# The second of the four late token sums, moved up to directly behind the first

## The chip, the cores and the metric

One core of a Trainium2 chip runs the whole kernel. The metric is the device time of one launch in microseconds (us). It is the median of several executions; one more execution was recorded by the hardware profiler, and all rows below come from that one.

## What is computed

One decoder layer on 512 tokens of width 2048, all in float32. The change lies where the gated MLP goes from its up projection to its down projection:

```
x = x + rmsnorm(token_mixer(rmsnorm(x, g1)), g2)
h = rmsnorm(x, g3)
up = h @ w_ffn_in                     # 512 x 11264: a | b, 5632 columns each
a  = conv_w[0]*a[t-2] + conv_w[1]*a[t-1] + conv_w[2]*a[t] + conv_b
f  = (gelu(a) * b) @ w_ffn_out        # 5632 -> 2048
y  = x + rmsnorm(f, g4)
```

## The kernel before, in words

**Products.** Each float32 operand is split into a high and a low part of a reduced type, and each product is three TensorE matmuls (high by high, high by low, low by high). Both projections of the MLP also use a Winograd-Strassen scheme: a 2 x 2 block product is made from seven products of sums of blocks, with the segments x0, z0, y0, z1, x1, y1 and y2. Each segment is two granules of 512 KB of weights. `granule` (line 129) splits one on ScalarE (line 138) and VectorE (line 139).

**Token sums.** The left operands of the seven down products are blocks of the hidden activations (a11, a12, a22) and four sums of them: s5 = a21 - a22, s2 = s5 - a11, s7 = a11 - a21, s3 = s2 - a12. They are made per group of 512 hidden columns by `token_sums`: each sum is one VectorE instruction (line 1373) on 128 x 512 float32, followed by a "put", a 256 KB transfer from the SyncE queue into DRAM (the tensors sd0 to sd4, line 48 is the helper that issues it). The four results share a tag with two buffers, and s2 reads s5, s3 reads s2. Nine groups make all four at once; the tenth group, whose sums are wanted last (they belong to sd4), keeps them as `late_sums`, to be made in the change-over.

**The change-over.** From the last up unit u to the first down units d0 and d1 the order is written out by hand in `change_over`: d0 x0, then u's y1, x1, y2, then d0's z0, y0, z1, x1, then d1's x0, then d0's y1 and y2, two granules each. `run_in_order` walks the granules. It makes a granule's halves two or three granules ahead, issues its matmuls (lines 1400 to 1402), after the second granule reads the banks out into acc (line 1406 on ScalarE, line 1408 on VectorE), and then runs the "hooks" of that granule: steps hung on a place with `at`. TensorE, ScalarE, VectorE and GpSimd keep program order here; where on its queue SyncE issues a transfer, and where instructions of the code behind the change-over (d1's z0 and its helpers at lines 1263 and 1281) are slotted in, a planner decides at build time from its own estimates.

y1 and y2 of d0 add into the same PSUM banks. So the first matmul of y2 has to wait until the read-out of y1 (two instructions at line 1408, one for each bank) is through.

**The late sums.** The four late sums hang, in the order s5, s2, s7, s3, on four places: d0 y0 first granule, d0 x1 second granule, d1 x0 first granule, d1 x0 second granule (lines 1541 and 1542).

Of the kernel before, what the change touches and what calls it, by code (L numbers as in the profile page):

```python
# [35 lines left out]
def hybrid_layer(ctx: ExitStack, tc: tile.TileContext, x, attn_pre_norm, w_in, w_alpha_up, b_alpha,  # L36
# [1416 lines left out]
    def at(u, seg, g, *fs):  # L1453
        hooks.setdefault((u, seg, g), []).extend(fs)

    def load_unit(u):
        u.t = [load_t(u.block(0, 0, g), u.a) for g in range(2)]
        u.b22, u.b21 = [], []

    def load_b(u, name, i, j, by=None):  # L1460
        getattr(u, name).extend(load(u.block(i, j, g), u.a, by) for g in range(2))

    def add_t(u, name, g):
        tt(u.t[g], u.t[g], getattr(u, name)[g], ALU.add)
# [13 lines left out]
    def prepare_at(c, n, load_at, split_at):  # L1478
        f, g = prepare_parts(c, n)
        at(*load_at, f)  # L1480
        at(*split_at, g)
# [41 lines left out]
    def change_over(u):  # L1523
        d0, d1 = downs[:2]
        order = [(d0, "x0"), (u, "y1"), (u, "x1"), (u, "y2")]
        order += [(d0, g) for g in ("z0", "y0", "z1", "x1")] + [(d1, "x0"), (d0, "y1"), (d0, "y2")]
        at(d0, "x0", 0, lambda: load_b(d0, "b22", 1, 1))
        at(d0, "x0", 0, late_tiles)
        at(d0, "x0", 1, lambda: (add_t(u, "b21", 0), add_t(u, "b21", 1)))
        at(u, "x1", 1, lambda: load_b(d0, "b21", 1, 0))  # L1530
        at(d0, "z0", 1, lambda: load_unit(d1))
        prepare_at(0, "s2", (d0, "x0", 1), (u, "y2", 0))
        prepare_at(0, "s3", (u, "y1", 1), (d0, "z0", 0))
        prepare_at(0, "a12", (u, "x1", 0), (d0, "z0", 1))
        prepare_at(0, "s7", (u, "x1", 1), (d0, "y0", 1))
        prepare_at(0, "a22", (u, "y2", 0), (d0, "z1", 1))
        for g in range(2):
            at(u, "y2", g, lambda g=g: add_t(d0, "b22", g))
        at(d0, "z1", 0, lambda: add_t(d0, "b21", 0))
        at(d0, "x1", 0, lambda: add_t(d0, "b21", 1))  # L1540
        for where in ((d0, "y0", 0), (d0, "x1", 1), (d1, "x0", 0), (d1, "x0", 1)):
            at(*where, lambda: late_sums.pop(0)())
        return order

    order = change_over(ups[-1])
    u = ups[-1]
    u.b21 = [load(u.block(1, 0, g), u.a) for g in range(2)]
# [217 lines left out]
```

## Time and profile before

| what | us |
|---|---|
| median of three executions | 2078.37 |
| lowest and highest of the three | 2074.48 and 2079.25 |
| the profiled execution, its own time | 2077.34 |
| its span in the profile | 2075.6 |
| PE (TensorE matmul) busy | 2048.7 |
| DVE (VectorE) busy | 1508.4 |
| ACT (ScalarE) busy | 1000.0 |

The profiled execution took 1.7 us more than its span. In the rows PE is TensorE, PEld its weight loads, DVE VectorE, ACT ScalarE, POOL GpSimd and SP SyncE; SPq and POOLq are the queues in which those issue transfers. L1373 is line 1373 of the kernel. A bracket at the end of a row of the timeline gives the idle time before the instruction and what ended it.

### The profile page before, as it was taken

Reading aid. Unit: us, or ns where it says so; the run is one execution under the profiler, and the core shown is the slowest. Engines: PE = TensorE matmul, PEld = TensorE weight load, DVE = VectorE, ACT = ScalarE, POOL = GpSimd, SP = SyncE. Lnnn points to the kernel's source line nnn. Section 1 sums busy time; section 2 is a strip of 40 time slices with the busy share of each in tenths; the row PEclk is TensorE's granted clock in tenths of the full one; section 3 lists DMA queues with packets and bytes.
Section 4 is the critical chain, followed back from the end, with each engine's and each line's share of the span. In section 5 each row is a group of like instructions: output and inputs, shape, how many; then the busy total and the mean of one; then the engine's idle time right before and its main releaser. Section 6 shows DMA issues by size and latency. Waiting matters only on the chain.

```text
span 2075.6 us, 35519 instructions
## 1 busy us (share of the span) xinstructions
PE 2048.7 (99%) x14429; PEld 1896.9 (91%) x14429; DVE 1508.4 (73%) x1793; ACT 1000.0 (48%) x1303; POOL 291.9 (14%) x306
## 2 busy tenths in 40 slices
PE   7999999999999999999999999999999999999998
PEld 6799999999988889899999999999999978888886
DVE  5967777666762255977777777777777888988977
ACT  5544444455552243454554554454455654544433
POOL 0112222222200000011011011111110111111100
PEclk9999999999999999999999999999999999999999
DMA  5488888888883354457667578577667886776663
GB/s 213 121 187 185 192 197 182 196 174 200 193 259 125 94 177 146 124 112 197 149 148 195 142 163 191 131 171 179 141 162 196 214 237 185 188 196 182 165 181 122
DMA packets 281465, 358.61 MB, mean 173 GB/s; under 512 B 14848, under 2 KB 223156, under 8 KB 279380
## 3 DMA queue, kind: packets, MB, share of 16 engines
q1 hardware_dynamic: 192148, 259.85, 37.4%
q0 software_dynamic: 84800, 94.38, 30.1%
q10 hardware_dynamic: 4352, 2.10, 0.4%
q8 instruction: 113, 1.85, 0.4%
q14 instruction: 52, 0.43, 0.1%
HBM read 311.72 MB, written 44.56 MB: 172 GB/s over the span
## 4 chain that ended last, share of the span: by engine, by line
PE 93%; DVE 2%; DMA 2%; issue 1%; ACT 1%; POOL 1%; DVEq 0%; SPq 0%; POOLq 0%; ACTq 0%
PE bank L1298 12%; PE bank L1299 12%; PE bank L1300 12%; PE bank L1400 6%; PE bank L1401 6%; PE bank L1402 6%; PE bank L193 3%; PE bank L192 3%; PE bank L194 3%; PE bank L793 3%; PE bank L795 3%; PE bank L794 3%; PE bank L797 2%; PE bank L798 2%; PE bank L799 2%; PE bank L176 2%
## 5 line engine op out<-in xcount | busy, mean ns | idle before, releaser
L138 ACT ACTIVATE ring<-raw 128x1024 fp32r<-128x1024 f32 x315 | 333.7, 1061 | 499.1 <-PE bank L1299 113.1
L139 DVE TENSOR_TENSOR ring<-raw,ring 128x1024 fp32r<-128x1024 f32 x315 | 383.5, 1223 | 259.3 <-ACT ring L138 256.0
L138 ACT ACTIVATE ring<-rt 128x1024 fp32r<-128x1024 f32 x221 | 234.5, 1061 | 259.3 <-PE bank L1299 154.0
L1299 PE MATMUL bank<-al,ring 128*128 128x256 f32 x1280 | 354.0, 277 | 0.0
L1298 PE MATMUL bank<-ah,ring 128*128 128x256 f32 x1280 | 354.0, 277 | 0.0
L1300 PE MATMUL bank<-ah,ring 128*128 128x256 f32 x1280 | 353.9, 277 | 0.0
L139 DVE TENSOR_TENSOR ring<-rt,ring 128x1024 fp32r<-128x1024 f32 x221 | 270.2, 1223 | 91.2 <-ACT ring L138 90.2
L1298 PEld LDWEIGHTS bank<-ah,ring 128*128 128x128 f32 x1280 | 240.5, 188 | 0.1
L1299 PEld LDWEIGHTS bank<-al,ring 128*128 128x128 f32 x1280 | 240.4, 188 | 0.1
L1300 PEld LDWEIGHTS bank<-ah,ring 128*128 128x128 f32 x1280 | 240.4, 188 | 0.0
L1402 PE MATMUL bank<-ring,al 128*128 128x512 f32 x424 | 165.8, 391 | 0.0
L1401 PE MATMUL bank<-ring,ah 128*128 128x512 f32 x424 | 165.7, 391 | 0.0
L1400 PE MATMUL bank<-ring,ah 128*128 128x512 f32 x424 | 153.2, 392 | 2.2 <-DVE acc L1408 2.2
L193 PE MATMUL bank<-ring,ah 128*128 128x512 f32 x280 | 109.8, 393 | 0.0
L192 PE MATMUL bank<-ring,ah 128*128 128x512 f32 x280 | 109.6, 397 | 0.0
L194 PE MATMUL bank<-ring,al 128*128 128x512 f32 x280 | 109.3, 393 | 0.0
L1246 POOL DMA_DIRECT2D raw<-in_w_ffn_in_dram x40 | 51.2, 1309 | 396.4 <-DVE ring L139 396.4
L1400 PEld LDWEIGHTS bank<-ring,ah 128*128 128x128 f32 x424 | 79.9, 188 | 19.7 <-DVE acc L1408 3.1
L1246 POOL DMA_DIRECT2D rt<-in_w_ffn_in_dram x40 | 50.9, 1279 | 325.9 <-DVE ring L139 303.4
L1402 PEld LDWEIGHTS bank<-ring,al 128*128 128x128 f32 x424 | 79.9, 189 | 16.7
L1401 PEld LDWEIGHTS bank<-ring,ah 128*128 128x128 f32 x424 | 79.9, 188 | 16.4
L797 PE MATMUL bank<-ring,ah 128*128 128x256 f32 x320 | 92.1, 288 | 1.0 <-ACT ah L151 1.0
(378 smaller groups left out, 5661.8 us busy)
## 6 DMA issues: line engine op xcount, KB each, us to landing
raw<-in_w_ffn_in_dram SPq DMA_DIRECT2D x96, 512.0 KB, 4.8
raw<-in_w_in_dram SPq DMA_DIRECT2D x56, 512.0 KB, 4.5
raw<-in_w_ffn_out_dram SPq DMA_DIRECT2D x46, 512.0 KB, 6.0
raw<-in_w_in_dram POOLq DMA_DIRECT2D x40, 512.0 KB, 7.2
rt<-in_w_ffn_in_dram SPq DMA_DIRECT2D x40, 512.0 KB, 6.1
rt<-in_w_ffn_in_dram POOLq DMA_DIRECT2D x40, 512.0 KB, 6.2
raw<-in_w_ffn_in_dram POOLq DMA_DIRECT2D x40, 512.0 KB, 6.9
raw<-in_w_o_dram SPq DMA_DIRECT2D x32, 512.0 KB, 3.9
```

The costliest lines, as they stand in the source:

```text
L138: act(hi, raw, AF.Copy)
L139: tt(lo, raw, hi.bitcast(F32), ALU.subtract)
L192: mm(banks[t], ah[:, t, s, :], w[0][:, k, :], start=st, stop=False)
L193: mm(banks[t], ah[:, t, s, :], w[1][:, k, :], start=False, stop=False)
L194: mm(banks[t], al[:, t, s, :], w[0][:, k, :], start=False, stop=sp)
L797: mm(o, sh[:, n, kk, :], wh[:, k, :], start=st, stop=False, **NOW)
L1298: mm(o, wh, sh[:, :, kk, :], start=start and kk == 0 and n == 0, stop=False, **NOW)
L1299: mm(o, wh, sl[:, :, kk, :], start=False, stop=False, **NOW)
L1300: mm(o, wl, sh[:, :, kk, :], start=False, stop=kk == HK - 1, **NOW)
L1400: mm(b[j], sh[:, o:o + P], w[0][:, q, :], start=start and st == 0, stop=False, **NOW)
L1401: mm(b[j], sh[:, o:o + P], w[1][:, q, :], start=False, stop=False, **NOW)
L1402: mm(b[j], sl[:, o:o + P], w[0][:, q, :], start=False, stop=st == 3, **NOW)
```

## The change

One place in one list is another: the second late sum, s2 = s5 - a11, with its put, hangs behind the first granule of d0's y0, where the first late sum hangs too, instead of behind the second granule of d0's x1. In the list of granules that is from place y0 1 to place x1 2; four whole granules lie between the two places. The third and the fourth late sum stay where they were. No instruction is added or removed.

```
-        for where in ((d0, "y0", 0), (d0, "x1", 1), (d1, "x0", 0), (d1, "x0", 1)):
+        for where in ((d0, "y0", 0), (d0, "y0", 0), (d1, "x0", 0), (d1, "x0", 1)):
             at(*where, lambda: late_sums.pop(0)())
```

## Rows read from the trace of the kernel before

**Rows 1.** The page, engines: busy us, share of the span, instructions.

```profile
PE 2048.7 (99%) x14429; PEld 1896.9 (91%) x14429; DVE 1508.4 (73%) x1793; ACT 1000.0 (48%) x1303; POOL 291.9 (14%) x306
```

**Rows 2.** Waits of PE over the run: us in total, times, longest.

```profile
PE bank L1400 <- DVE acc L1408: 2.2, 1, 2.2
PE bank L797 <- ACT ah L151: 1.0, 1, 1.0
```

**Rows 3.** Chain that ended last, 1676 to 1692: start, us, what.

```profile
1670.02 7.93 DMA sd4s<-s
...
1678.04 0.13 DVE s L1373
...
1679.79 0.69 DVE acc L1408
...
1685.18 0.39 PE bank L1400
...
1687.19 0.23 PE bank L1402
```

**Rows 4.** Stretches of 2 us: busy of each engine, granted clock, DMA share, GB/s.

```profile
1682.00:1684.00 2.00, 1.99 (x5) 1.46 (x5) 2.00 (x3) 0.00 (x0) 0.00 (x0) 0.50 0.86 316
```

**Rows 5.** Timeline of VectorE, 1652 to 1679: start, length, line, operation.

```profile
1652.83 0.69 DVE L1373 TENSOR_TENSOR s<-u 128x512 f32<-128x512 f32 x1
1654.95 1.23 DVE L152 TENSOR_TENSOR al<-st,ah 128x1024 fp32r<-128x1024 f32 x1 [1.44 <-ACT ah L151]
...
1667.57 0.69 DVE L1373 TENSOR_TENSOR s<-s,u 128x512 f32<-128x512 f32 x1
1668.17 1.22 DVE L139 TENSOR_TENSOR ring<-raw,ring 128x1024 fp32r<-128x1024 f32 x1
1669.31 0.68 DVE L1373 TENSOR_TENSOR s<-u 128x512 f32<-128x512 f32 x1
...
1673.55 1.23 DVE L139 TENSOR_TENSOR ring<-rt,ring 128x1024 fp32r<-128x1024 f32 x1 [1.29 <-ACT ring L138]
1678.04 0.69 DVE L1373 TENSOR_TENSOR s<-s,u 128x512 f32<-128x512 f32 x1 [3.27 <-DMA sd4s<-s]
```

**Rows 6.** Timeline of the SyncE queue: transfers issued, 1656 to 1671.

```profile
1656.21 0.32 SPq L48 DMA_DIRECT2D st<-sd1a  x1
...
1668.28 0.34 SPq L48 DMA_DIRECT2D sd4s<-s  x1
1669.42 0.37 SPq L102 DMA_DIRECT2D raw<-in_w_ffn_out_dram  x1
1670.02 0.34 SPq L48 DMA_DIRECT2D sd4s<-s  x1
```

**Rows 7.** Transfer issued at 1669.42: KB, us to landing.

```profile
raw<-in_w_ffn_out_dram SPq DMA_DIRECT2D x1, 512.0 KB, 7.9
```

**Rows 8.** Regular group: third put issued, KB and landing; fourth sum.

```profile
1575.79 0.32 SPq L48 DMA_DIRECT2D sd4s<-s  x1
...
sd4s<-s SPq DMA_DIRECT2D x1, 256.0 KB, 5.3
...
1581.23 0.69 DVE L1373 TENSOR_TENSOR s<-s,u 128x512 f32<-128x512 f32 x1 [2.12 <-DMA sd4s<-s]
```

**Rows 9.** SyncE's data queue in 1664:1665, 1675:1676: packets, MB, share.

```profile
q1 hardware_dynamic: 12, 0.02, 5.4%
...
q1 hardware_dynamic: 217, 0.41, 106.9%
```

**Rows 10.** Timeline of PE: first matmul of d0 z0, first matmul behind the gap.

```profile
1642.12 0.39 PE L1400 MATMUL bank<-ring,ah 128*128 128x512 f32 x1
...
1680.52 0.50 PE L1400 MATMUL bank<-ring,ah 128*128 128x512 f32 x1 [2.21 <-DVE acc L1408]
```

**Rows 11.** GpSimd's accumulating load issued at 1653.21, landing; its reader.

```profile
raw<-in_w_ffn_out_dram POOLq DMA_DIRECT2D x1, 512.0 KB, 11.0
...
1664.31 1.06 ACT L138 ACTIVATE ring<-raw 128x1024 fp32r<-128x1024 f32 x1 [1.67 <-PE bank L1402]
```

## The prediction, made before the changed kernel was run

> **What bounds the kernel now.** I read the page's engine totals first: TensorE is busy for 99% of the span [rows 1], so only what stands on its way can matter. Next the waits of TensorE over the whole run: behind the start-up its longest wait is 2.2 us, in the change-over, where the first matmul of d0's y2 waits for the read-out of y1 on VectorE; the next is 1.0 us, in another stage [rows 2, 10]. Third, the chain of work that ended last, at that place. It says where the wait comes from: the put issued at 1670.02 lands 7.93 us later, at 1677.95; at 1678.04 the fourth late sum starts on VectorE; behind it in VectorE's order stands the read-out of y1 at 1679.79; at 1680.52 TensorE goes on [rows 3, 10]. The timeline of VectorE shows the same from the other side: it stood for 3.27 us in front of the fourth sum [rows 5].
>
> So the stretch costs TensorE this much. Its matmuls stop at 1680.52 - 2.21 = 1678.31 [rows 10]. In the chain thirteen matmuls follow, from 1680.52 to 1685.18 + 0.39 = 1685.57 [rows 3, 10]: 5.05 us, where thirteen at the pace of 0.23 us, which the chain has again by 1687.19 [rows 3], take 2.99. The granted clock was 0.50 in 1682 to 1684, the lower of its two levels, 1.2 GHz [rows 4]. Gap and slow matmuls together are 2.2 + 2.1 = 4.3 us. That is the most that any cure of this stall can give, and it is 0.21% of the time. About 0.2% is also what a measurement of this kernel can tell from no change.
>
> **Whose landing is waited for.** This decides the case. SyncE issued the second put at 1668.28 and the third at 1670.02 [rows 6], and the chain names the one at 1670.02 [rows 3], that is the third late sum's, s7. The regular group before shows the same: its third put is issued at 1575.79 and takes 5.3 us, to 1581.1, and its fourth sum starts at 1581.23 after a wait of 2.12 [rows 8]. The code agrees. Four sums share two buffers, and the fourth, s3, reads the second, s2; so s2's buffer can't be handed out while s3 is still to be made, and s3 gets the buffer of s7 and has to wait for s7's put. The change moves s2 and its put, and not s7's. The wait stays; the question is what the move does to its length.
>
> **The change part by part.**
> *The sum on VectorE, new place.* s2 takes 0.69 us. Behind the first sum (1652.83 + 0.69 = 1653.52) VectorE stands idle for 1.44 us, until ScalarE hands it the next step at 1654.95 [rows 5]. s2 fits into that: cost 0. Without this cover it would be 0.60 us (the start-to-start distance from s2 to its successor, 1667.57 to 1668.17 [rows 5]) on a VectorE that has idle time again at 1673.55 [rows 5], thus still nothing for TensorE.
> *Its put, new place.* The sum is done by about 1653.52 + 0.69 = 1654.2, and SyncE can issue the put then. The next transfer on that queue came at 1656.21 [rows 6], so nothing is held up behind it: cost 0 on the queue.
> *The sum on VectorE, old place.* At 1667.57 0.60 us falls away. The next split there has had its input from ScalarE since 1664.31 + 1.06 = 1665.37 [rows 11], so it moves up, and s7 with it, from 1669.31 to 1668.71; its put is issued at about 1669.4 instead of 1670.02 [rows 5, 6].
> *The landing of s7's put.* The load issued at 1669.42 landed 7.9 us later, at 1677.3 [rows 7], and s7's put at 1677.95 [rows 3]: 0.63 us apart. At the 0.41 MB per us that this queue moved in 1675 to 1676 [rows 9], its 0.26 MB need 0.64 us. So the landings follow each other at the queue's pace, and an earlier issue alone gives nothing; but the second put's 0.26 MB, which stood in front, are gone from there, 0.64 us. Lower bound of this gain: 0, since the same bytes now go at 1654 to 1657, beside an accumulating load [rows 11], and if all 16 engines are full from there on, everything behind is later by as much and nothing is won. Upper bound: 0.64, if a hole takes them up. There is one: in 1664 to 1665 SyncE's queue moved only 0.02 MB [rows 9]. Whether the engines were free for more just then, the row does not say, so I take half: 0.3 us.
>
> The skill has a rule that speaks against the move. The Trainium skill (DMA: Bandwidth & Descriptors, section on queues, rings and completion order) says that each DMA engine takes turns, packet by packet, between the queues that have work. By it the moved put takes turns from the accumulating load beside it. The sum would be 0 instead of -0.3 by that rule alone; no row before can show this case.
>
> That load, issued at 1653.21, landed after 11.0 us, at 1664.2, and ScalarE read it at 1664.31 [rows 11]: no slack there. But VectorE takes the result at 1668.17 [rows 5], 2.8 us after ScalarE is done with it, or 2.2 us after s2 has left. A delay of up to 0.64 us ends in that slack and costs 0.
> *TensorE's cover.* From the start of d0's z0 at 1642.12 [rows 10] there are twelve granules to the end of y1 (z0, y0, z1, x1, d1's x0, y1), of twelve matmuls each: 144 x 0.23 = 33.1 us, to 1675.2. Until 1678.31 TensorE works at something else: 3.1 us that can only be d1's z0, slotted in ahead of y2 by the planner, whose own estimate must have y2 waiting there. With s7 0.60 us earlier in its estimate, it may slot in less: between 0 and 0.60 us of cover lost. What is not slotted in there is done later, so the loss is real: when TensorE goes on is set by VectorE, and then there is more left to do. I take half again, 0.3 us.
>
> **Sum.** -0.3 (landing) + 0.3 (cover) = 0.0, bounds -0.64 and +0.60. One more bound: the gap would be 2.2 - 0.64 = 1.6 us at best, and no row has a gap between 1.0 us and the 2.2 us that were followed by 1.2 GHz. If the clock stays up behind 1.6, another 2.1 us are won: -2.7 in all. 1.6 lies as near to the one as to the other, and it is the best case for the gap, so I keep this as a bound only.
>
> Against the profiled execution's own time, 2077.34 us (its span, 2075.6, and 1.7 around it), the forecast is 2077.3. That execution lies 1.0 below the median of the three runs, 2078.37; the middle of all four is 2077.9, and I forecast that.
>
> **The rivals.**
> *The whole stall goes (faster).* If s3 waited for s2's put and not for s7's, the change would remove the wait: s2's put would have landed ten us before. VectorE would go on with s3 at 1673.55 + 1.23 = 1674.8, the read-out would be at 1674.8 + (1679.79 - 1678.04) = 1676.5, over by 1677.2, before TensorE's work runs out at 1678.31. Gain 4.3: 2073.6. For it: both puts are in flight in front of s3, and the waits are inferred. Against it: the time of the wait's end, which fits the third put within 0.1 us in both groups [rows 3, 8], while s2's put stood ahead of a load that had landed by 1677.3 [rows 6, 7]. Chance 9%.
> *The cover goes (slower).* The planner sees s2 and its put out of the way, estimates that y2 can start at once, and places all 3.1 us of z0 behind it. TensorE then stands from 1675.2 to about 1680.2, 5.0 us instead of 2.2, and ends up 3.1 - 0.3 = 2.8 later; the stretch at 1.2 GHz, which costs 2.1 us now, would cost up to as much again. Together +2.8 to +4.9; with the gap more than doubled I take the upper part, +4.4: 2082.3. It decides from 0.3 us of lost cover on (below that the sooner landing pays for it), and passes the bound of 0.2% only with nearly all of it. For it: the planner did slot work in there. Against it: VectorE still has s3 behind s7's put in its order, so its estimate should keep a wait. Chance 8%.
> *Nothing at all moves.* The sum must stand where its hook stands, as VectorE keeps program order, so the move itself is sure; but if the queues give and take the same, the time is 2077.9 like the forecast, and it is counted there.
>
> **How the numbers follow.** Forecast with its bounds (-2.7 to +0.6) 83%, whole stall gone 9%, cover gone 8%. Faster by over 0.2% (4.2 us): the whole stall gone, 9%, and 2% for the forecast's low end with the scatter of runs on top: 11%. Slower 8%. Within 81%. The range: the forecast's bounds are 2075.2 and 2078.5. The three runs of before reach from 3.4 below to 1.4 above the middle that I used, so a median may lie off by about half of that again: 2074.2 to 2080.0. The two rivals' own times, 2073.6 and 2082.3, stay outside, 17% in all.
>
> **What would show it.** In the changed profile: s2 directly behind s5 at about 1653.5, and the idle time behind it cut from 1.44 to some 0.8; s7 near 1668.7; the fourth sum still behind an idle stretch, ended by a put of sd4 that was issued next to s7, landing at 1677.3 to 1677.9; TensorE's wait for line 1408 between 1.6 and 2.8 us, and the half clock behind it. The forecast is wrong if the fourth sum has no wait (then I took the wrong buffer), if TensorE's wait is over 4 us (then the cover went), or if a new wait stands in the stages behind, where TensorE has none now [rows 2].

## The result, and the profile after

The changed kernel takes 2081.02 us (median of 17 runs, 2077.97 to 2087.72), the kernel before 2076.39 us beside it (17 runs, 2073.03 to 2079.38). The ratio is 1.0023, with a 95% interval from 1.0014 to 1.0031: slower by 0.23%. The forecast was no change, 2077.9 us, with a range to 2080.0.

The profiled execution of the changed kernel is the slowest of its 17, 2087.72 us. Some 7 us of its excess lie ahead of the change: its first late sum starts at 1659.81, in the profile of before at 1652.83 [rows 5], with the same instructions up to there. A second profile of the same kernel (e5 below) doesn't have them, so all readings here are distances inside the change-over.

The waits of TensorE over the run (in total, times, longest):

```profile
PE bank L159 <- DVE xt L248: 10.4, 2, 9.5
PE bank L1401 <- DVE ring L139: 5.7, 1, 5.7
PE bank L1300 <- DVE ring L139: 4.5, 9, 0.8
```

The 2.2 us wait for the read-out of y1 at line 1408 [rows 2, 10] is gone. In its place stands one of 5.7 us, for something else: line 139, the low half of a granule of weights. (The 4.5 us at line 1300 are in the up projection, ahead of the change.) The timeline of TensorE, before and behind the gap:

```profile
1681.95 0.61 PE L1400 MATMUL bank<-ring,ah 128*128 128x512 f32 x2
1688.29 0.79 PE L1401 MATMUL bank<-ring,ah 128*128 128x512 f32 x1 [5.72 <-DVE ring L139]
```

1681.95 is 22.14 us behind the first late sum. In the profile of before the same two matmuls stand 22.15 us behind it:

```profile
1674.98 0.62 PE L1400 MATMUL bank<-ring,ah 128*128 128x512 f32 x2
```

They are the first two of d1's z0. So TensorE now stops right at the start of z0, which was the work that covered for it before. These two matmuls take the high half of the weights and run; the next one takes the low half. The timeline of VectorE says why that is late:

```profile
1659.81 0.68 DVE L1373 TENSOR_TENSOR s<-u 128x512 f32<-128x512 f32 x1
1660.53 0.69 DVE L1373 TENSOR_TENSOR s<-s,u 128x512 f32<-128x512 f32 x1
1661.93 1.22 DVE L152 TENSOR_TENSOR al<-st,ah 128x1024 fp32r<-128x1024 f32 x1 [0.71 <-ACT ah L151]
...
1675.68 0.68 DVE L1373 TENSOR_TENSOR s<-u 128x512 f32<-128x512 f32 x1
1676.28 1.21 DVE L139 TENSOR_TENSOR ring<-rt,ring 128x1024 fp32r<-128x1024 f32 x1
1677.59 1.23 DVE L152 TENSOR_TENSOR al<-st,ah 128x1024 fp32r<-128x1024 f32 x1
1685.28 0.69 DVE L1373 TENSOR_TENSOR s<-s,u 128x512 f32<-128x512 f32 x1 [6.46 <-DMA sd4s<-s]
1685.88 1.22 DVE L139 TENSOR_TENSOR xlo<-rt,xhi 128x1024 fp32r<-128x1024 f32 x1
1687.02 1.22 DVE L139 TENSOR_TENSOR ring<-rt,ring 128x1024 fp32r<-128x1024 f32 x1
1688.15 1.28 DVE L1408 TENSOR_TENSOR acc<-acc,bank 128x512 f32<-128x512 f32 x2
```

The second sum stands directly behind the first, in what was idle time. The third starts 15.87 us behind the first, before it was 16.48. But the row at 1673.55 of before, a split at line 139 ahead of the fourth sum [rows 5], is missing there: it stands behind the fourth sum now, at 1687.02, with one more split between them. It is the low half of the first granule of d1's z0. The fourth sum still waits for a put, 6.46 us instead of 3.27, and z0's low half waits behind it. (Some 3 us of the longer wait are only that nothing stands between it and the step at 1677.59 any more.) In the built programs TensorE, ScalarE and GpSimd have the same order before and after. SyncE's differs in the second put alone. VectorE's differs in the second sum, in this split, and in two steps of line 1263 behind it. Nobody wrote this exchange: z0 belongs to the code behind the change-over, which the planner slots in.

The put that the fourth sum waits for, in the SyncE queue and in the chain of work that ended last:

```profile
1676.39 0.34 SPq L48 DMA_DIRECT2D sd4s<-s  x1
...
1676.39 8.79 DMA sd4s<-s
```

It is again the third put, issued 16.58 us behind the first sum (before 17.19 [rows 5, 6]), and it landed 8.79 us later, at 1685.18.

Last, the clock. Rows are stretches of 2 us: length, then busy time of TensorE, its weight loads, VectorE, ScalarE and GpSimd, granted clock, DMA share, GB/s:

```profile
1684.00:1686.00 2.00, 0.00 (x0) 0.00 (x0) 0.72 (x2) 0.00 (x0) 0.00 (x0) 0.81 1.03 410
1686.00:1688.00 2.00, 0.00 (x0) 0.00 (x0) 2.00 (x2) 0.00 (x0) 0.00 (x0) 0.50 0.89 264
1688.00:1690.00 2.00, 1.71 (x4) 1.42 (x5) 2.00 (x4) 0.00 (x0) 0.00 (x0) 0.50 0.94 324
1690.00:1692.00 2.00, 2.00 (x6) 1.52 (x6) 2.00 (x3) 0.00 (x0) 0.00 (x0) 0.50 0.46 178
```

The clock falls while TensorE still stands. TensorE comes back at 1.2 GHz and stays there for some 4 us. Before, it came back at the full clock and fell to 1.2 GHz some 1.5 us later [rows 4, 10].

### The profile page after: what moved, and what is told of

Same layout as the page of the kernel before. It is cut to its first block, busy times and chain, and to the rows that moved or that the text cites. A ratio compares the mean times of both kernels' runs of the same rounds, so it can differ in the third digit from the quotient of the medians.

```text
span 2086.0 us, 35516 instructions
## 1 busy us (share of the span) xinstructions
PE 2052.0 (98%) x14429; PEld 1898.1 (91%) x14429; DVE 1505.9 (72%) x1793; ACT 998.5 (48%) x1303; POOL 292.0 (14%) x306
## 4 chain that ended last, share of the span: by engine, by line
PE 49%; issue 16%; DVE 3%; DMA 2%; POOL 2%; ACT 1%; DVEq 0%; POOLq 0%; ACTq 0%
PE bank L1401 6%; PE bank L1402 6%; PE bank L1400 6%; PE bank L1300 6%; PE bank L1298 6%; PE bank L1299 6%; PE bank L193 3%; PE bank L192 3%; PE bank L194 3%; PE bank L176 1%; PE bank L175 1%; PE bank L174 1%; DVE ring L139 1%; DMA rt<-in_w_ffn_in_dram 1%; POOL rt L1246 1%
```

## The experiments

Three theories were on trial. Theory 1: the loss is the planner's new order on VectorE, z0's low half behind a sum that waits. Theory 2: it is the traffic of the moved put. Theory 3: it lies in the up projection. The yardstick in the traces is the **stretch** from the first late sum to the same step behind the change-over, a split at line 152 behind some 2.4 us of idle VectorE. In the kernel before it runs from 1652.83 [rows 5] to the first of these rows, in the changed kernel from 1659.81 to the second:

```profile
1698.07 1.23 DVE L152 TENSOR_TENSOR al<-st,ah 128x1024 fp32r<-128x1024 f32 x1 [2.46 <-ACT ah L151]
...
1708.46 1.23 DVE L152 TENSOR_TENSOR al<-st,ah 128x1024 fp32r<-128x1024 f32 x1 [2.46 <-ACT ah L151]
```

That is 45.24 and 48.65 us. All runs (the kernel before was run beside each; gaps and stretches are from one profile each):

| kernel | TensorE's gap, us | stretch, us | median, us (before beside it) | ratio, 95% interval |
|---|---|---|---|---|
| before | 2.2 | 45.24 | | |
| the change | 5.7 | 48.65 | 2081.02 (2076.39) | 1.0023, 1.0014 to 1.0031 |
| e5, the change again | 4.6 | 48.70 | 2080.24 (2077.22) | 1.0013, 1.0005 to 1.0022 |
| e1, order restored | 1.5 | 43.09 | 2075.64 (2077.27) | 0.9996, 0.9985 to 1.0006 |
| e2, put at its old place | 1.9 | 43.47 | 2076.35 (2077.27) | 0.9995, 0.9987 to 1.0004 |
| e6, before, low half behind the sum | 4.8 | 47.90 | 2080.61 (2077.22) | 1.0015, 1.0006 to 1.0023 |
| e3, before, own buffer | none | 40.89 | 2073.19 (2077.27) | 0.9981, 0.9971 to 0.9991 |
| e4, the change, own buffer | none | 40.89 | 2072.86 (2077.27) | 0.9981, 0.9971 to 0.9992 |
| e7, before, fourth sum later | none | 40.89 | 2074.21 (2077.22) | 0.9983, 0.9975 to 0.9992 |

**e1, the order on VectorE restored.** One edge is added to the changed kernel: the fourth sum is issued behind the low half of z0's first granule. (`sum_ops` and `lo_ops` collect the instructions of lines 1373 and 139; `issue_order` stands for the class of an edge that fixes the order of issue and adds no wait. `n_lo` is the number of low halves made ahead of z0. The lines that collect are left out here and below.)

```
-    downs[1].z0(held=True)
+    n_lo = len(lo_ops); downs[1].z0(held=True)
+    tc.add_manual_dep(sum_ops[NG - 1, "s3"].ins, lo_ops[n_lo].ins.name, issue_order)
```

> The changed kernel with one thing put back: the low half of the first granule of d1's z0 goes ahead of the fourth late sum on VectorE again, as before. The second sum and its put stay at their new places. Theory 1 (the planner's new order on VectorE is the cause): TensorE's gap falls from 5.7 us to between 2.2 and 2.8 (2.2 as before, up to 0.3 more as the third put took 8.8 us instead of 7.9), and it waits for the read-out of y1 (line 1408) again; the time is that of the kernel before within 0.1%, some 4 us below the changed kernel. Theory 2 (the moved put's traffic is the cause): the gap and the time stay with the changed kernel, +0.15 to +0.3% over before. Theory 3 (the loss sits in the up projection, where the changed profile shows 4.5 us of small waits): also +0.15 to +0.3%.

The built program is that of before but for the second sum and its put. Against the changed kernel, TensorE, ScalarE, GpSimd and SyncE have the same order, and VectorE alone differs. The loss is gone: 2075.64 us, ratio 0.9996. VectorE around the fourth sum, TensorE behind its gap, and the stretch of 2 us in which it goes on:

```profile
1670.67 1.23 DVE L139 TENSOR_TENSOR ring<-rt,ring 128x1024 fp32r<-128x1024 f32 x1 [1.72 <-ACT ring L138]
1674.47 0.69 DVE L1373 TENSOR_TENSOR s<-s,u 128x512 f32<-128x512 f32 x1 [2.58 <-DMA sd4s<-s]
...
1676.95 0.50 PE L1400 MATMUL bank<-ring,ah 128*128 128x512 f32 x1 [1.52 <-DVE acc L1408]
...
1676.00:1678.00 2.00, 1.05 (x5) 0.87 (x6) 2.00 (x4) 0.07 (x1) 0.00 (x0) 1.00 1.04 358
```

The low half is ahead of the sum, and TensorE's gap is back at line 1408, 1.52 us long: shorter than expected. The order of the transfers is the same as in the change, so theory 2 falls, and with the same up projection theory 3 falls too.

**e2, only the put held back.** The changed kernel, with one edge on the SyncE queue: the second put is issued behind the third of the four loads for d1, where it was before. (`put_ops` and `ld_ops` collect the puts and the loads; `n_ld` is the number of loads ahead of these four.)

```
+    tc.add_manual_dep(put_ops[NG - 1, "s2"].ins, ld_ops[n_ld + 2].ins.name, issue_order)
```

> The changed kernel with only the put of the second sum held back to its old place on the SyncE queue (behind three of the four loads for d1); the sum itself stays directly behind the first. At build the planner then keeps VectorE's order of before. Theory 1: gap 2.2 us as before, time of the kernel before within 0.1%; it shows that the put, not the sum, made the planner change the order. Theory 2 (traffic of the moved put): also as before, so e1 tells the two apart. Theory 3: +0.15 to +0.3%.

```profile
1674.32 1.23 DVE L139 TENSOR_TENSOR ring<-rt,ring 128x1024 fp32r<-128x1024 f32 x1 [1.72 <-ACT ring L138]
1678.52 0.69 DVE L1373 TENSOR_TENSOR s<-s,u 128x512 f32<-128x512 f32 x1 [2.97 <-DMA sd4s<-s]
...
1681.00 0.50 PE L1400 MATMUL bank<-ring,ah 128*128 128x512 f32 x1 [1.92 <-DVE acc L1408]
```

No edge touches VectorE here, and still the planner keeps the low half ahead of the fourth sum, as before. The gap is 1.9 us at line 1408 (2.2 were expected), the ratio 0.9995. So the exchange comes with the put's new place, not with the sum's. What the planner reckoned for the two puts can't be read from a trace. That it sees the third put land sooner when the second is out of its way, and therefore the fourth sum ready ahead of z0's low half, is the argument that fits, and not more than that.

**e5, the change again.** The changed kernel as it is.

> The changed kernel as it is, once more, for a second profile. Theory 1 (planner's order): TensorE waits 5 to 6 us for the low half of d1's z0 (line 139) in the change-over, the fourth sum stands behind some 6 us of idle VectorE, and the stretch from the first late sum to the same step after the change-over takes 3 to 4 us more than the 45.2 us of before. Theory 3 (up projection): the 4.5 us of small waits in the up projection, at line 1300, show again; if they are chance, they are mostly gone and the time is 0.15 to 0.3% over before all the same.

```profile
PE bank L1401 <- DVE ring L139: 4.6, 1, 4.6
...
1675.96 0.69 DVE L1373 TENSOR_TENSOR s<-s,u 128x512 f32<-128x512 f32 x1 [5.37 <-DMA sd4s<-s]
1676.57 1.22 DVE L139 TENSOR_TENSOR xlo<-rt,xhi 128x1024 fp32r<-128x1024 f32 x1
1677.70 1.22 DVE L139 TENSOR_TENSOR ring<-rt,ring 128x1024 fp32r<-128x1024 f32 x1
```

The waits at line 1300 are not there any more, so they were chance; the wait for line 139 is. The gap is 1.1 us shorter than in the first profile (the put took 7.69 us instead of 8.79), and yet the stretch is the same, 48.70. The clock made up the difference. It is low from some 1678.3 to 1685.1 here, as its means in the first and the last of these stretches show:

```profile
1678.00:1680.00 2.00, 1.02 (x3) 0.84 (x4) 2.00 (x3) 0.00 (x0) 0.00 (x0) 0.57 1.03 362
...
1684.00:1686.00 2.00, 2.00 (x8) 1.59 (x7) 1.23 (x1) 0.70 (x1) 0.00 (x0) 0.72 0.00 0
```

TensorE was back at 1678.98, so it worked at 1.2 GHz for some 6 us, in the first profile for some 4. The gap missed the lower end of the expectation (5 us) by 0.4.

**e6, the exchange without the moved sum.** The kernel before, second sum at its old place, with the opposite edge: z0's low half behind the fourth sum.

```
+    tc.add_manual_dep(lo_ops[n_lo].ins, sum_ops[NG - 1, "s3"].ins.name, issue_order)
```

> The kernel before, with the low half of d1's z0 held behind the fourth late sum on VectorE, where the changed kernel has it; nothing else is moved by hand, but the planner now also places d1's z0 behind y2 on TensorE. Theory 1: the order alone, with the second sum at its old place, makes the loss: TensorE's gap is 5 to 5.6 us (3.1 us of cover gone, 2.2 to 2.5 as before), 2.5 to 5 us over the kernel before, +0.1 to +0.25%. If the moved sum or put is needed for the loss: within 0.1% of before.

A loss of that size comes without the moved sum and put: ratio 1.0015, 2.66 us in the stretch. But the program is not the changed kernel's in all: the planner changes TensorE's order too. Only the first two matmuls of z0 stand ahead of y2 here, the next twelve behind the first six of y2. So TensorE waits for line 1408, with nothing to cover it, for 4.8 us (5 to 5.6 were expected). e6 alone can't part the order on VectorE from that on TensorE; e1, where TensorE's order is the same as in the change, does.

```profile
PE bank L1400 <- DVE acc L1408: 4.8, 1, 4.8
...
1679.40 0.69 DVE L1373 TENSOR_TENSOR s<-s,u 128x512 f32<-128x512 f32 x1 [5.67 <-DMA sd4s<-s]
```

**e3 and e4, a buffer of its own for the fourth sum.** In the kernel before (e3) and in the changed one (e4), the fourth late sum takes a buffer of a tag that is free in the change-over.

```
-  t = made[n] = fp.tile([P, 2, 256], F32, name=n, tag="sum", bufs=2)
+  t = made[n] = fp.tile([P, 2, 256], F32, name=n, tag="p1" if (gi, n) == (NG - 1, "s3") else "sum", bufs=2)
```

> The kernel before, with a buffer of another tag (free at that time) for the fourth late sum, so that it has no put to wait for. If the fourth sum waits for its buffer, that is for the third put, as the prediction says: no idle time in front of the fourth sum, no gap of TensorE in the change-over, full clock there, and 4.3 us less than before: 2072, -0.2%. If the wait is for something else: gap and time as before.

> The changed kernel with the same extra buffer for the fourth sum. By theory 1 the new place of the second sum costs nothing of its own: no gap, and the time of e3 within 0.1% (2072). If moving the sum or its put costs something beside the wait (theories 2 and 3): above e3 by 2 to 5 us.

VectorE in e3, from the third to the fourth sum and on to the read-out of y1:

```profile
1670.72 0.69 DVE L1373 TENSOR_TENSOR s<-u 128x512 f32<-128x512 f32 x1
1671.33 1.22 DVE L139 TENSOR_TENSOR ring<-rt,ring 128x1024 fp32r<-128x1024 f32 x1
1672.46 0.69 DVE L1373 TENSOR_TENSOR s<-s,u 128x512 f32<-128x512 f32 x1
...
1676.47 1.28 DVE L1408 TENSOR_TENSOR acc<-acc,bank 128x512 f32<-128x512 f32 x2
```

No wait in front of the fourth sum and no gap of TensorE in the change-over. The stretch is 40.89 us in both, 4.35 less than before: the stall was priced at 4.3. So the wait was for a buffer of the sums' tag. That it is the third sum's and not the second's, the change shows: there the second put was issued and landed like this,

```profile
1661.25 0.32 SPq L48 DMA_DIRECT2D sd4s<-s  x1
DMA to landing us min/median/max: 7.5/7.5/7.5
```

so at 1668.8, and still the fourth sum waited to 1685.28, 0.1 us behind the landing of the third. Since e4 is as fast as e3, the second sum costs nothing that can be seen at its new place once nobody waits behind it. (On TensorE e3 has the order of before; in e4 two matmuls of z0 move behind the first six of y2.)

**e7, the fourth sum later.** The kernel before, with the fourth late sum hung behind the second granule of d0's y1.

```
-  for where in ((d0, "y0", 0), (d0, "x1", 1), (d1, "x0", 0), (d1, "x0", 1)):
+  for where in ((d0, "y0", 0), (d0, "x1", 1), (d1, "x0", 0), (d0, "y1", 1)):
```

> The kernel before, with the fourth late sum hung two granules later (d0 y1 first granule in place of d1 x0 second granule), with two buffers as before: the planner puts it behind the read-out of y1 on VectorE. By theory 1 the wait for the third put then holds up nothing TensorE needs: no gap in the change-over, the time of e3 within 0.1% (-0.2%, 2073). If the fourth sum's wait still stood in front of other work that TensorE waits for, a gap of 1 to 3 us would remain.

Two granules later than d1's x0 second granule is the second of y1, not the first as the expectation has it. And the place behind the read-out is not the planner's choice: the hooks of a second granule run behind its read-out, and VectorE keeps program order here.

```profile
1674.80 1.28 DVE L1408 TENSOR_TENSOR acc<-acc,bank 128x512 f32<-128x512 f32 x2
1678.02 0.69 DVE L1373 TENSOR_TENSOR s<-s,u 128x512 f32<-128x512 f32 x1 [1.94 <-DMA sd4s<-s]
```

The wait is still there, 1.94 us, but the read-out of y1 is through before it, and TensorE waits for nothing in the change-over. (Two matmuls of z0 stand as in e4.) The stretch is 40.89 as with a buffer of its own, and two buffers are enough. e3, e4 and e7 are all faster than the kernel before by more than their intervals.

## Why the prediction was wrong

**Right: what bounds, and whose landing is waited for.** The stall was priced at 4.3 us; e3, e4 and e7 gave 4.35 in the stretch and 3.0 to 4.4 between the medians. The fourth sum waits for its buffer and so for the third put: moving the second put left the wait there, and another buffer took it away. The rival "the whole stall goes" fell for the reason given.

**Right: the second sum on VectorE.** It fits into the idle time (1.44 us became 0.71), and the third sum comes 0.61 us sooner, forecast 0.60.

**Open in size: the landing of the third put.** Forecast 0.3 us sooner, bounds 0 and 0.64. Counted from the first late sum it landed at 25.12 us before, and with the second put at its new place at 25.37 (the change), 24.27 (e5) and 24.43 (e1); with the second put at its old place, at 24.83 (e2) and 25.01 (e6). Single landings of one program lie 1.1 us apart, so 0.3 can't be seen. The hole that the upper bound rested on was no idle time: SyncE's queue moved little in 1664 to 1665 [rows 9], but the 16 DMA engines were full, as the stretch of the kernel before shows (DMA share 1.11):

```profile
1664.00:1665.00 1.00, 1.00 (x6) 0.81 (x5) 1.00 (x2) 0.69 (x1) 0.52 (x1) 1.00 1.11 205
```

The rule of the Trainium skill that was weighed there (DMA: Bandwidth & Descriptors, section on queues, rings and completion order), as the prediction reads it, would have it at 0, and these landings can't tell that from 0.3. The prediction says that the sum would be 0 by that rule; it is this term that would be 0, and the sum +0.3.

**The step that failed: TensorE's cover.** The prediction took it that a sooner third sum in the planner's estimate would change how many matmuls of z0 are slotted in ahead of y2 on TensorE, 0 to 0.60 us. TensorE's order did not change at all. What changed is VectorE's, where z0 has an instruction too: the split at 1673.55 stood in rows 5, directly ahead of the waiting sum, and was read as a fixed neighbour. It was as free as the matmuls, and worth more. With the split ahead of the sum, z0 covers 3.1 us of the wait. With the split behind the sum there is no cover: the gap is 5.7 or 4.6 us, and the stretch 3.4 us longer. e1 shows that this is the cause: with VectorE's order alone put back, the loss is gone. The prediction's sum had +0.3 in the place of that. Its own sign that the cover went, a wait of TensorE over 4 us, came in both profiles.

**The range.** It doesn't follow from its working: half of 3.4 and half of 1.4 around 2075.2 and 2078.5 make 2073.5 to 2079.2, not 2074.2 to 2080.0. The measured 2081.02 lies above either.

**The rival that came nearest.** "The cover goes" had the place right and nearly the price, +2.8 to +4.9 with 4.4 taken, against 3.4 in the stretch, 4.6 between the medians of the first comparison and 3.0 of the second. It had the mechanism wrong. It let the planner think that y2 could start at once and move the matmuls behind it, and was given 8% because VectorE's wait should have kept it from that. e6 comes close to that case, with all but two of these matmuls behind the first six of y2, and costs 2.66 us in the stretch. In the change the matmuls stayed where they were and lost their operand.

**The clock.** The lower bound of the forecast, -2.7, rested on the clock staying up behind a shorter gap. It did: in e1 and e2, behind gaps of 1.5 and 1.9 us, the granted clock was 1.00 in every stretch of 2 us. e1's stretch is 2.15 us shorter than before, of which 0.7 is gap. That is a single profile each, and the medians of e1 and e2 don't differ from before beyond their intervals, so no gain of that kind is shown.

## What to carry to other kernels

When an in-order engine waits for a transfer, look at what stands directly behind the waiting instruction, and ask of each neighbour whether the order is written down or was picked by a planner: what was picked can change places when a transfer moves in some other queue. Compare the order of the built programs, engine by engine, before explaining a time. And cure the wait itself (a buffer that is free, or a later place for a result that nobody needs yet) rather than move what stands next to it: that took the whole stall, 0.17 to 0.19%, where the move lost 0.13 to 0.23%.

## What the runs showed of the hardware

A put of 256 KB, in the same program and at the same place in the queues, landed 8.79 us after its issue in one execution and 7.69 in another, with the DMA engines full (shares of 1.03 and more in most stretches of 2 us). In one profile each, behind gaps of TensorE of 1.5 and 1.9 us the granted clock stayed at 2.4 GHz; behind 2.2 us and more it went to 1.2 GHz, in the profile of before some 1.5 us after work had begun again [rows 4, 10], in the change, e5 and e6 while TensorE still stood. So a stall has two prices: e5's gap was 1.1 us shorter than that of the first profile, and its stretch was no shorter at all.
